# Scan of a gated DeltaNet: QK loaded later and multiplied on GpSimd, KK's beta, the state's decay and the inverse's factor in full width on GpSimd

## The chip, the core and the metric

The kernel runs on one core of a Trainium2 chip. Its engines run side by side, each with its own queue of instructions: TensorE (PE; its weight loads are shown apart as PEld), VectorE (DVE), ScalarE (ACT), GpSimd (POOL), and SyncE (SP), whose queue issues the DMA transfers here. The metric is device time in microseconds (us), the median of several runs. The profile is one further execution, with its own time.

## The reference

One layer of a diffusion backbone, for 128 context tokens and 2048 latent tokens of width 1024. An adaptive RMSNorm feeds one input projection; half of its outputs go through a bidirectional gated DeltaNet with 4 heads of 128, the other half through a gated spatial MLP; an output projection, a residual, a second norm and a squared-ReLU MLP of width 4096 follow. The change lies in the DeltaNet. For each chunk of tokens, direction and head (g is the running sum of the log decays in the chunk, S the state):

```python
decay = where(incl, exp(g[:, None] - g[None, :]), 0)
a_mat = where(strict, (k * beta) @ k.T * decay, 0)
sol   = solve(a_mat + I, concat([v * beta, k * beta * exp(g)]))   # gives u and w
qk    = (q @ k.T) * decay
# one step of the scan:
v_new = u - w @ S
o     = (q * exp(g)) @ S + qk @ v_new
S     = S * exp(g_last) + (k * exp(g_last - g)).T @ v_new
```

## The kernel before, in words

The 2176 tokens are 17 tiles of 128. A first part projects all tiles and writes to DRAM what the scan needs: the keys and queries in both layouts (`kT_d`, `kt_d`, `qT_d`), twice the values (`vt_d`), and the products K K^T (`kk_d`) and K Q^T (`qk_d`) of each tile. Small tables stay in SBUF, a column per tile, direction and head: `beta`, `hbeta` (half of beta), `gcol` (g), `egl` (exp of the last g), `eglg` (exp of the last g less g) and `neg2` (-2 exp g).

The second part is the scan. It has 34 units, 17 tiles forward and then 17 backward, each over one tile of 128 tokens (the kernel takes the tile as the chunk) and all four heads at once, so that a working tile is 128 x 4 x 128, that is 128x512. A unit has two halves.

- The preparation (`prep`, 17 steps) makes the inverse. E is the matrix of decays: ScalarE takes absolute differences of g (L1019) and an exponential (L1020); GpSimd selects the strict triangle Es (L1022) and the inclusive one E (L1024). VectorE multiplies KK by beta and Es, one head at a time (L1032), and GpSimd sets the diagonal to one (L1034). AH and AL are the 16-bit parts of the result. X and Y are the inverse and its transpose, which five levels (block sizes 2 to 32) build up: in each, four small matmuls (L1064), VectorE's masked copy P (L1068), eight small matmuls (L1076, L1078), and ScalarE's two copies to Y and X (L1079, L1080). In the second step of the first level VectorE multiplies QK by E (L1082). A last level and a correction R (L1114) follow, and ScalarE copies the result T from PSUM with the factor half beta, one head at a time (L1123).
- The scan proper (`scan`, 4 steps) is serial from unit to unit through the state S. Step 1: S times kT, which VectorE scales by `neg2` and adds to vt (L1135), and S times qT, which ScalarE scales by `neg2` into o (L1127). Step 2: T times vt; VectorE makes vs with `eglg` (L1148) and ScalarE the copy vn (L1150). Step 3: kt times vs; VectorE makes the new state, S times `egl` plus the product, one head at a time (L1162). Step 4: QK times vn; VectorE joins it with o times -0.5 (L1179, and in the backward pass also with the forward output `of`, L1181).

Between these stand long matmuls that don't depend on the scan, the "fill": in the forward pass the projections of the gated MLP, with GELU and statistics on ScalarE and VectorE; in the backward pass the output projection, its normalisation, and the operands of the later MLP (tiles `opH`, `opL`, L888 and L889). Both need an inverse square root now and then, a power on GpSimd (L183: `rs` in the forward pass, `rr` and `r` in the backward one), with VectorE ahead of it (L182) and behind it.

Each step has a due time in units, a number that `at` and `spread` give it from the list `WINDOWS`; the steps are emitted in the order of these times, and extra edges (`emit`) keep fill matmuls behind those of the chain. The framework then puts each engine's instructions in one order with a planner that has costs of its own. On the chip every engine takes its own in that order, and an instruction that waits holds up those behind it. `prep_loads` (due three units ahead) loads g, KK and QK; `scan_loads` (one unit ahead) loads kt, kT, vt and qT. A tile comes from a ring of buffers with a tag; a load waits until the last reader of its buffer is done. KK, E and Es share one ring of four (`s32`); QK has three of its own; kt, kT, vt, qT and S two each.

The third part is the MLP, some 5,600 long matmuls back to back; the change doesn't touch it.

Of the kernel before, what the change touches and what calls it, by code (L numbers as in the profile page):

```python
# [8 lines left out]
F32 = mybir.dt.float32  # L9
# [3 lines left out]
AF = mybir.ActivationFunctionType  # L13
# [4 lines left out]
P = 128  # L18
# [3 lines left out]
NT = 17  # L22
# [41 lines left out]
def hybrid_step(  # L64
# [53 lines left out]
    make_identity(nc, ident)  # L118
    ident16 = cp.tile([P, P], F16, name="ident16")
    V.tensor_copy(ident16, ident)  # L120
    nhalf = cp.tile([P, 80], F32, name="nhalf")
    V.memset(nhalf, -0.5)
    zcol = cp.tile([P, KT], F32, name="zcol")
    V.memset(zcol, 0.0)
# [31 lines left out]
    neg2 = cp.tile([P, NT, 8], F32, name="neg2")  # L156
    eglg = cp.tile([P, NT, 8], F32, name="eglg")
    egl = cp.tile([P, NT, 8], F32, name="egl")
    vec = cp.tile([P, 73], F32, name="vec")
    a1 = cp.tile([P, 2, KT], F32, name="a1")  # L160
    b1 = cp.tile([P, 2, KT], F32, name="b1")
# [118 lines left out]
    with ExitStack() as ph:  # L280
# [365 lines left out]
        def decay_steps():  # L646
# [46 lines left out]
            def f3():  # L693
                pl = pt()
                T.matmul(pl[:, 0:136], ones, s8(6).rearrange("p t c -> p (t c)"), start=True, stop=True)
                pl3 = pl[:, 0:136].rearrange("p (t c) -> p t c", c=8)
                A.activation(egl, pl3, AF.Exp)
                V.scalar_tensor_tensor(out=eglg, in0=gcol, scalar=-1.0, in1=pl3, op0=ALU.mult, op1=ALU.add)
                A.activation(eglg, eglg, AF.Exp)
                A.activation(neg2, gcol, AF.Exp)  # L700
                V.tensor_scalar_mul(neg2, neg2, -2.0)

            def f4():
                gflat = gcol.rearrange("p t c -> p (t c)")
# [240 lines left out]
    with ExitStack() as ph:  # L945
# [39 lines left out]
        def unit(t, d):  # L985

            u = {}
            sg = 1 if d == 0 else -1

            def col(tab, h):  # L990
                return tab[:, t, d * 4 + h : d * 4 + h + 1]

# [4 lines left out]
            def prep_loads():  # L997
                u["gb"] = load_rows(g_d, t, d)
                u["KK"] = s32("KK")
                load(out=u["KK"], in_=kk_d[t])  # L1000
                u["QK"] = q32("QK", 3)
                load(out=u["QK"], in_=qk_d[t])

            def scan_loads():
                for nm, src in (("kt", kt_d), ("kT", kT_d), ("vt", vt_d), ("qT", qT_d)):
                    u[nm] = q32(nm, 2)
                    if nm in ("kT", "qT"):
                        load(out=u[nm], in_=src[t])
                    else:
                        load(out=u[nm], in_=src[t * P : (t + 1) * P, :].rearrange("p (h d) -> p h d", h=H))  # L1010

            prep = []
            scan = []

            @prep.append
            def _():
                e = s32("E")
                for h in range(H):
                    A.activation(e[:, h, :], u["gb"][:, h, :], AF.Abs, scale=-1.0, bias=col(gcol, h))  # L1019
                A.activation(e, e, AF.Exp, scale=-1.0)  # L1020
                es = s32("Es")
                G.affine_select(out=es, in_=e, pattern=[[0, 4], [-sg, P]], compare_op=ALU.is_gt, fill=0.0,  # L1022
                                base=0, channel_multiplier=sg)
                G.affine_select(out=e, in_=e, pattern=[[0, 4], [sg, P]], compare_op=ALU.is_ge, fill=0.0,  # L1024
                                base=0, channel_multiplier=-sg)
                u["Es"], u["E"] = es, e

            @prep.append
            def _():
                a = u["KK"]  # L1030
                for h in range(H):
                    V.scalar_tensor_tensor(out=a[:, h, :], in0=a[:, h, :], scalar=col(beta, h),  # L1032
                                           in1=u["Es"][:, h, :], op0=ALU.mult, op1=ALU.mult)
                G.affine_select(out=a, in_=a, pattern=[[0, 4], [1, P]], compare_op=ALU.not_equal, fill=1.0,  # L1034
                                base=0, channel_multiplier=-1)
                u["AH"], u["AL"], u["X"] = f16("AH", BA), f16("AL", BA), f16("X", BX)
                A.copy(u["AH"], a)
                V.tensor_tensor(out=u["X"], in0=u["AH"], in1=bc4(bd2), op=ALU.mult)
# [10 lines left out]
            def level(s):  # L1049
# [20 lines left out]
                @prep.append  # L1070
                def _():
                    p = pd()
                    py, px = packed(p, 0), packed(p, 1)
                    y, x, pm = half(u["Y"], yi), half(u["X"], 1 - yi), half(u["P"], yi)
                    for h in range(H):
                        T.matmul(py[:, h], u["X"][:, h, :], pm[:, h], start=True, stop=True)  # L1076
                    for h in range(H):
                        T.matmul(px[:, h], u["P"][:, h, :], x[:, h], start=True, stop=True)  # L1078
                    A.copy(y, py)  # L1079
                    A.copy(x, px)  # L1080
                    if s == 2:
                        V.tensor_tensor(out=u["QK"], in0=u["QK"], in1=u["E"], op=ALU.mult)  # L1082

            for s in (2, 4, 8, 16, 32):
                level(s)
# [31 lines left out]
            @prep.append  # L1117
            def _():
                p = pd()
                quad(p, u["X"], u["R"])  # L1120
                u["T"] = q32("T", BT)
                for h in range(H):
                    A.activation(u["T"][:, h, :], p[:, h, :], AF.Copy, scale=col(hbeta, h))  # L1123

            def scaled(out, p, table):
                for h in range(H):
# [3 lines left out]
            def _():  # L1130
                if u["s"] is not None:
# [5 lines left out]
                    p = pd()  # L1137
                    quad(p, u["qT"], u["s"])
                    u["o"] = q32("o", 2)
                    scaled(u["o"], p, neg2)  # L1140

            @scan.append
            def _():
                p = pd()
                quad(p, u["T"], u["vt"])
                u["vs"] = q32("vs", 1)
                cols = eglg[:, t, d * 4 : d * 4 + 4].unsqueeze(2).to_broadcast([P, 4, P])
                V.tensor_tensor(out=u["vs"], in0=p, in1=cols, op=ALU.mult)  # L1148
                u["vn"] = q32("vn", BT)
                A.copy(u["vn"], p)  # L1150

            @scan.append
            def _():
                s = u["s"]
                p = pd()
                quad(p, u["kt"], u["vs"])
                sn = q32("S", 2)
                if s is None:
                    A.copy(sn, p)
                else:  # L1160
                    for h in range(H):
                        V.scalar_tensor_tensor(out=sn[:, h, :], in0=s[:, h, :], scalar=col(egl, h),  # L1162
                                               in1=p[:, h, :], op0=ALU.mult, op1=ALU.add)
                u["sn"] = sn

            @scan.append
            def _():
# [8 lines left out]
                        V.tensor_tensor(out=o, in0=p, in1=of, op=ALU.add)  # L1176
                else:
                    o = u["o"]
                    V.scalar_tensor_tensor(out=o, in0=o, scalar=-0.5, in1=of if d else p, op0=ALU.mult, op1=ALU.add)  # L1179
                    if d:  # L1180
                        V.tensor_tensor(out=o, in0=o, in1=p, op=ALU.add)  # L1181
                if d == 0:
                    store(out=of_d[t * P : (t + 1) * P, :].rearrange("p (h d) -> p h d", h=H), in_=o)

            u["t"], u["d"] = t, d
            u["prep"], u["scan"] = prep, scan
            u["prep_loads"], u["scan_loads"] = prep_loads, scan_loads
            return u

        units = [unit(t, 0) for t in range(NT)] + [unit(t, 1) for t in [0] + list(range(NT - 1, 0, -1))]  # L1190
# [205 lines left out]
        for i, u in enumerate(units):  # L1396
            w = p2 if i <= NT else p3
            at(i - 3 if i > PL else -10, u["prep_loads"])
            at(i - 1, u["scan_loads"])
            n = len(u["prep"])  # L1400
            for j, st in enumerate(u["prep"]):
                at(i - w[0] + (j + 0.5) * (w[0] - w[1]) / n, st, "prep")
# [556 lines left out]
```

## Time and profile before

| | |
|---|---|
| Median of 3 runs | 2599.12 us (2596.32 to 2601.89) |
| Profiled execution | 2598.87 us, its span 2596.8 us, granted TensorE clock 0.995 |
| First part | 0 to about 440 us |
| Scan, forward pass | about 440 to 880 us |
| Scan, backward pass | about 880 to 1250 us |
| MLP | about 1250 to 2597 us |

A row of a group reads: line, engine, operation, output<-inputs by the program's names, output shape<-input shape, count | busy us, mean ns of one | idle us of the engine just before them, and what ended most of it. A row of waits reads: who waited, for whom, us in total, times, the longest. A row of the timeline reads: start, duration, engine, line, operation, and in brackets the idle time before it and what ended it. Busy matmuls are pipelined, and their ends are modelled. "Busy" of a group merges what overlaps.

### The profile page before, as it was taken

Reading aid. Unit: us, or ns where it says so; the run is one execution under the profiler, and the core shown is the slowest. Engines: PE = TensorE matmul, PEld = TensorE weight load, DVE = VectorE, ACT = ScalarE, POOL = GpSimd, SP = SyncE. Lnnn points to the kernel's source line nnn. Section 1 sums busy time; section 2 is a strip of 40 time slices with the busy share of each in tenths; the row PEclk is TensorE's granted clock in tenths of the full one; section 3 lists DMA queues with packets and bytes.
Section 4 is the critical chain, followed back from the end, with each engine's and each line's share of the span. In section 5 each row is a group of like instructions: output and inputs, shape, how many; then the busy total and the mean of one; then the engine's idle time right before and its main releaser. Section 6 shows DMA issues by size and latency. Waiting matters only on the chain.

```text
span 2596.8 us, 44648 instructions
## 1 busy us (share of the span) xinstructions
PE 2553.3 (98%) x15508; PEld 2156.5 (83%) x15508; DVE 1801.0 (69%) x3733; ACT 1220.9 (47%) x3048; POOL 228.8 (9%) x448
## 2 busy tenths in 40 slices
PE   9999999899999999999999999999999999999998
PEld 5999999688888787778888888888888888888887
DVE  5867756766667878886678876666665557784874
ACT  4755555554555667764355643332342432243441
POOL 3112212111111111210000000000000000000000
PEclk9999999899999999999999999999999999999999
DMA  8977738645445657885768789444479979786773
GB/s 288 304 212 214 209 109 266 201 148 154 154 144 166 208 173 248 275 275 181 279 204 256 224 283 307 114 118 118 123 234 370 334 268 321 270 256 213 236 247 106
DMA packets 494695, 571.88 MB, mean 220 GB/s; under 512 B 35124, under 2 KB 297564, under 8 KB 490886
## 3 DMA queue, kind: packets, MB, share of 16 engines
q1 hardware_dynamic: 494470, 569.04, 68.2%
q8 instruction: 122, 2.00, 0.3%
q14 instruction: 103, 0.84, 0.1%
HBM read 389.23 MB, written 179.67 MB: 219 GB/s over the span
## 4 chain that ended last, share of the span: by engine, by line
PE 87%; DVE 5%; DMA 4%; ACT 1%; issue 1%; POOL 0%; SPq 0%; DVEq 0%; POOLq 0%; ACTq 0%
PE f L226 16%; PE f L228 16%; PE f L227 16%; PE pj L226 7%; PE pj L228 7%; PE pj L227 7%; PE pd L995 5%; PE f L1599 2%; PE pm L226 1%; PE pm L227 1%; PE pm L228 1%; PE pt L610 1%; PE pt L569 1%; DMA QK<-qk_d 1%; PE pd L1076 1%
## 5 line engine op out<-in xcount | busy, mean ns | idle before, releaser
L226 PE MATMUL f<-hop,zH 128*128 128x512 f32 x960 | 373.4, 389 | 1.2 <-ACT zH L1485 1.2
L228 PE MATMUL f<-hop,zL 128*128 128x512 f32 x960 | 373.4, 389 | 0.4 <-DVE zL L1479 0.4
L227 PE MATMUL f<-hop,zH 128*128 128x512 f32 x960 | 373.3, 389 | 0.0
L226 PE MATMUL f<-hop,wH 128*128 128x512 f32 x896 | 355.2, 397 | 0.3 <-DMA hop<-hop_d 0.3
L227 PE MATMUL f<-hop,wH 128*128 128x512 f32 x896 | 349.1, 390 | 0.0
L228 PE MATMUL f<-hop,wL 128*128 128x512 f32 x896 | 347.9, 390 | 0.0
L1485 ACT CAST zH<-zraw 128x512 fp32r<-128x512 f32 x240 | 147.2, 620 | 300.6 <-DMA zraw<-s_d 98.0
L226 PEld LDWEIGHTS f<-hop,zH 128*128 128x128 f32 x960 | 180.2, 188 | 39.2 <-ACT zH L1485 1.6
L228 PEld LDWEIGHTS f<-hop,zL 128*128 128x128 f32 x960 | 180.2, 188 | 38.5 <-DVE zL L1479 1.3
L227 PEld LDWEIGHTS f<-hop,zH 128*128 128x128 f32 x960 | 180.2, 188 | 37.6 <-issue 0.2
L1479 DVE TENSOR_TENSOR zL<-zraw,zH 128x512 fp32r<-128x512 f32 x240 | 162.8, 687 | 65.5 <-ACT zH L1485 51.0
L228 PEld LDWEIGHTS f<-hop,wL 128*128 128x128 f32 x896 | 168.2, 188 | 35.3
L226 PEld LDWEIGHTS f<-hop,wH 128*128 128x128 f32 x896 | 168.5, 188 | 33.0 <-issue 0.7
L227 PEld LDWEIGHTS f<-hop,wH 128*128 128x128 f32 x896 | 168.5, 188 | 32.4
L226 PE MATMUL pj<-kH,wH 128*128 128x386 f32 (+2 forms) x568 | 191.2, 339 | 1.2 <-ACT junk L586 1.1
L228 PE MATMUL pj<-kH,wL 128*128 128x386 f32 (+2 forms) x568 | 190.4, 336 | 0.0
L227 PE MATMUL pj<-kL,wH 128*128 128x386 f32 (+2 forms) x568 | 190.1, 336 | 0.1
L183 POOL TENSOR_TENSOR r<-rsq,nhalf 128x1 f32<-128x1 f32 (+1 forms) x38 | 25.5, 670 | 1428.8 <-DVE rsq L182 1428.8
L556 DVE SCALAR_TENSOR_TENSOR cv<-pj,vec,cv 128x384 f32<-128x384 f32 (+2 forms) x164 | 87.0, 539 | 53.5 <-ACT cv L553 52.2
L226 PEld LDWEIGHTS pj<-kH,wH 128*128 128x128 f32 x568 | 107.6, 190 | 4.3 <-issue 2.3
L227 PEld LDWEIGHTS pj<-kL,wH 128*128 128x128 f32 x568 | 108.0, 190 | 1.1 <-POOL kL L495 0.4
L1485 ACT CAST wH<-s 128x512 fp32r<-128x512 f32 x96 | 59.4, 621 | 104.8 <-DVE s L1479 102.9
(398 smaller groups left out, 5705.5 us busy)
## 6 DMA issues: line engine op xcount, KB each, us to landing
zraw<-z_d SPq DMA_DIRECT2D x212, 256.0 KB
raw<-in_w_ff_dram SPq DMA_DIRECT2D x128, 256.0 KB
hop<-hop_d SPq DMA_DIRECT2D x28, 1024.0 KB
z_d<-c SPq DMA_DIRECT2D x96, 256.0 KB
zraw<-s_d SPq DMA_DIRECT2D x96, 256.0 KB
raw<-in_w_mod_dram SPq DMA_DIRECT2D x80, 256.0 KB
r<-in_w_ff_dram SPq DMA_DIRECT2D x80, 256.0 KB
s_d<-s SPq DMA_DIRECT2D x64, 256.0 KB
```

The source lines that it names most:

```text
L183: G.tensor_tensor(out=out, in0=t[:np_, :n], in1=nhalf[:np_, :n], op=ALU.pow)
L226: T.matmul(ps, lh, rh, start=first and i == 0, stop=False, skip_group_check=more)
L227: T.matmul(ps, lh, rl, start=False, stop=False, skip_group_check=more)
L228: T.matmul(ps, ll, rh, start=False, stop=last and i == n - 1, skip_group_check=more)
L556: V.scalar_tensor_tensor(out=cv[:, o : o + m], in0=ps[:, s + sh : s + sh + m], scalar=convw[:, w, j : j + 1], in1=cv[:, o : o + m], op0=AL ...
L569: T.transpose(pq[:, i * P : (i + 1) * P], u["x2"][:, i * P : (i + 1) * P], ident)
L610: T.matmul(ps[:, i * P : (i + 1) * P], kTt[:, i * P : (i + 1) * P], rhs[:, i * P : (i + 1) * P], start=True, stop=True)
L995: T.matmul(p[:, h, :], lhs[:, h, :], rhs[:, h, :], start=True, stop=True)
L1076: T.matmul(py[:, h], u["X"][:, h, :], pm[:, h], start=True, stop=True)
L1479: V.tensor_tensor(out=out, in0=a, in1=b, op=op)
L1485: A.copy(h, src)
L1599: T.matmul(ps[:, c : c + P], self.raw[m, kh][:, kp, :], x0[kh][:, kp, :], start=first and kp == 0, stop=last and kp == 3)
```

## The change

- QK is loaded in `scan_loads`, one unit ahead and first in that group, instead of three units ahead, with two buffers instead of three.
- A new step `scale_loads`, due 0.6 units ahead, multiplies vt by half beta and QK by E, both on GpSimd. QK's product on VectorE in the first level of the inverse goes.
- KK is multiplied by beta on GpSimd in the first step of the preparation, ahead of Es; VectorE then multiplies it by Es in one instruction of full width instead of four.
- T is copied without a factor, in one ScalarE instruction instead of four; the factor is in vt, and in `neg2`, which becomes -2 exp(g) times half beta. A new table `egc` holds exp(g), with which o is scaled, so that the factor -0.5 in step 4 goes.
- The state's decay is a GpSimd product into the new state's buffer in step 2; step 3 then adds the matmul's result in one VectorE instruction instead of four.
- E has three buffers of its own, and the ring of four holds KK and Es alone.
- The constant `nhalf` is 104 columns wide instead of 80.

```diff
-    nhalf = cp.tile([P, 80], F32, name="nhalf")
+    nhalf = cp.tile([P, 104], F32, name="nhalf")
...
-                A.activation(neg2, gcol, AF.Exp)
-                V.tensor_scalar_mul(neg2, neg2, -2.0)
+                A.activation(egc, gcol, AF.Exp)
+                V.scalar_tensor_tensor(out=neg2, in0=egc, scalar=-2.0, in1=hbeta, op0=ALU.mult, op1=ALU.mult)
...
+            def times(out, src, tab):
+                cols = tab[:, t, d * 4 : d * 4 + 4].unsqueeze(2).to_broadcast([P, 4, P])
+                G.tensor_tensor(out=out, in0=src, in1=cols, op=ALU.mult)
...
                 load(out=u["KK"], in_=kk_d[t])
-                u["QK"] = q32("QK", 3)
+
+            def scan_loads():
+                u["QK"] = q32("QK", 2)
                 load(out=u["QK"], in_=qk_d[t])
-
-            def scan_loads():
...
+            def scale_loads():
+                times(u["vt"], u["vt"], hbeta)
+                G.tensor_tensor(out=u["QK"], in0=u["QK"], in1=u["E"], op=ALU.mult)
...
-                e = s32("E")
+                e = pp.tile([P, 4, P], F32, tag="E", name="E", bufs=3)
...
                 A.activation(e, e, AF.Exp, scale=-1.0)
+                times(u["KK"], u["KK"], beta)
...
-                for h in range(H):
-                    V.scalar_tensor_tensor(out=a[:, h, :], in0=a[:, h, :], scalar=col(beta, h),
-                                           in1=u["Es"][:, h, :], op0=ALU.mult, op1=ALU.mult)
+                V.tensor_tensor(out=a, in0=a, in1=u["Es"], op=ALU.mult)
...
-                    if s == 2:
-                        V.tensor_tensor(out=u["QK"], in0=u["QK"], in1=u["E"], op=ALU.mult)
...
-                for h in range(H):
-                    A.activation(u["T"][:, h, :], p[:, h, :], AF.Copy, scale=col(hbeta, h))
+                A.copy(u["T"], p)
...
-                    scaled(u["o"], p, neg2)
+                    scaled(u["o"], p, egc)
...
+                u["sn"] = q32("S", 2)
+                if u["s"] is not None:
+                    times(u["sn"], u["s"], egl)
...
-                    for h in range(H):
-                        V.scalar_tensor_tensor(out=sn[:, h, :], in0=s[:, h, :], scalar=col(egl, h),
-                                               in1=p[:, h, :], op0=ALU.mult, op1=ALU.add)
-                u["sn"] = sn
+                    V.tensor_tensor(out=sn, in0=sn, in1=p, op=ALU.add)
...
-                    V.scalar_tensor_tensor(out=o, in0=o, scalar=-0.5, in1=of if d else p, op0=ALU.mult, op1=ALU.add)
                     if d:
-                        V.tensor_tensor(out=o, in0=o, in1=p, op=ALU.add)
+                        V.tensor_tensor(out=o, in0=o, in1=of, op=ALU.add)
+                    V.tensor_tensor(out=o, in0=o, in1=p, op=ALU.add)
...
             at(i - 1, u["scan_loads"])
+            at(i - 0.6, u["scale_loads"])
```

More of the change, by code (lines that the diff above doesn't have):

```diff
@@ L158, in hybrid_step @@
     egl = cp.tile([P, NT, 8], F32, name="egl")
+    egc = cp.tile([P, NT, 8], F32, name="egc")
     vec = cp.tile([P, 73], F32, name="vec")
@@ L1156, in _ @@
                 quad(p, u["kt"], u["vs"])
-                sn = q32("S", 2)
+                sn = u["sn"]
                 if s is None:
@@ L1186, in unit @@
             u["prep"], u["scan"] = prep, scan
-            u["prep_loads"], u["scan_loads"] = prep_loads, scan_loads
+            u["prep_loads"], u["scan_loads"], u["scale_loads"] = prep_loads, scan_loads, scale_loads
             return u
```

## The prediction

> **What bounds the kernel now.** I read the page's engine summary first, then the table of stretches, then TensorE's waits inside the scan, and then went upstream from those waits. The first fence is the page, the second the table of stretches (us; busy time of PE, PEld, DVE, ACT, POOL; granted clock; DMA share; GB/s).
>
> ```profile
> span 2596.8 us, 44648 instructions
> PE 2553.3 (98%) x15508; PEld 2156.5 (83%) x15508; DVE 1801.0 (69%) x3733; ACT 1220.9 (47%) x3048; POOL 228.8 (9%) x448
> ```
>
> ```profile
> 480.00:880.00 400.00, 392.83 (x3399) 325.78 (x3398) 280.13 (x786) 214.26 (x583) 50.41 (x69) 1.00 0.52 160
> 880.00:1200.00 320.00, 303.76 (x2717) 251.28 (x2716) 260.11 (x650) 212.70 (x661) 52.70 (x59) 0.99 0.70 230
> 1200.00:1250.00 50.00, 50.00 (x314) 42.29 (x313) 31.51 (x74) 18.26 (x59) 3.45 (x3) 1.00 0.49 170
> 1250.00:2590.00 1340.00, 1336.41 (x6207) 1113.42 (x6205) 906.94 (x1478) 506.43 (x965) 16.06 (x25) 1.00 0.72 235
> ```
>
> TensorE is busy 98% of the span, and the MLP (1250 to 2590) is full. The change touches only the scan, 480 to 1250. There TensorE is idle 7.2 us in the forward pass (400 - 392.83) and 16.2 us in the backward pass (320 - 303.76). VectorE is busy 70% of the first and 81% of the second, ScalarE 54% and 66%, GpSimd 13% and 16%. So the change is worth what it takes from, or adds to, TensorE's waits, and nothing else. They are, from 440 to 1250 (total us, times, longest):
>
> ```profile
> PE pd L1076 <- DVE P L1068: 11.1, 13, 1.6
> PE pd L1064 <- ACT Y L1079: 8.1, 12, 1.5
> PE pd L995 <- issue: 2.4, 1, 2.4
> PE pm L227 <- DVE wL L201: 2.0, 1, 2.0
> PE pd L1076 <- DVE vt L1135: 1.4, 1, 1.4
> ```
>
> The matmuls of the inverse's levels wait 11.1 us for a VectorE product (P) and 8.1 us for a ScalarE copy (Y): 19.2 us in 25 waits, 0.7% of the kernel. That is the stake. Why P and Y are late shows the timeline of a typical stretch of the backward pass (start and duration in us; first VectorE, then ScalarE, then GpSimd and TensorE, whose brackets hold the idle time before):
>
> ```profile
> 1050.89 0.68 DVE L1082 TENSOR_TENSOR QK<-QK,E 128x512 f32<-128x512 f32 x1
> ...
> 1053.04 0.68 DVE L1179 SCALAR_TENSOR_TENSOR o<-o,of 128x512 f32<-128x512 f32 x1
> 1053.64 0.61 DVE L182 TENSOR_SCALAR rsq<-r 128x4 f32<-128x4 f32 x1
> 1054.26 0.81 DVE L1032 SCALAR_TENSOR_TENSOR KK<-KK,beta,Es 128x128 f32<-128x128 f32 x1
> 1054.99 0.68 DVE L889 TENSOR_TENSOR opL<-y,opH 128x512 fp32r<-128x512 f32 x1
> 1055.59 0.87 DVE L1032 SCALAR_TENSOR_TENSOR KK<-KK,beta,Es 128x128 f32<-128x128 f32 x3
> 1056.38 0.74 DVE L1068 TENSOR_TENSOR P<-pd,sm 128x256 f16<-128x256 f32 x2
> ```
>
> ```profile
> 1050.29 1.15 ACT L1123 ACTIVATE T<-pd,hbeta 128x128 f32<-128x128 f32 x4
> 1051.29 0.66 ACT L888 CAST opH<-y 128x512 fp32r<-128x512 f32 x1
> 1051.79 0.42 ACT L1079 CAST Y<-pd 128x256 f16<-128x256 f32 x1
> ```
>
> ```profile
> 1051.71 2.51 POOL L1022 TENSOR_SCALAR_AFFINE_SELECT Es<-E 128x512 f32<-128x512 f32 x1 [9.09 <-DVE QK L1082]
> 1052.27 0.28 PE L1064 MATMUL pd<-Y,AH 128*128 128x64 f16 x4 [0.81 <-ACT Y L1079]
> 1056.85 0.29 PE L1076 MATMUL pd<-P,X 128*128 128x64 f16 x4 [1.39 <-DVE P L1068]
> ```
>
> VectorE works without a gap here, and P stands at the end of the queue, behind two things that the change takes or shortens (QK at 1050.89, KK at 1054.26 and 1055.59). Y stands two places behind T on ScalarE.
>
> **The change, part by part.** The prices are these groups (mean ns of one behind the busy us):
>
> ```profile
> L1032 DVE SCALAR_TENSOR_TENSOR KK<-KK,beta,Es 128x128 f32<-128x128 f32 x136 | 45.8, 390 | 9.0 <-POOL Es L1022 7.2 <-DMA KK<-kk_d 1.7
> L1162 DVE SCALAR_TENSOR_TENSOR S<-S,egl,pd 128x128 f32<-128x128 f32 x128 | 35.8, 340 | 9.6 <-PE pd L995 9.5
> L1082 DVE TENSOR_TENSOR QK<-QK,E 128x512 f32<-128x512 f32 x34 | 23.5, 690 | 31.9 <-DMA QK<-qk_d 29.0 <-POOL E L1024 2.7
> L1148 DVE TENSOR_TENSOR vs<-pd,eglg 128x512 f32<-128x512 f32 x34 | 23.1, 679 | 5.5 <-PE pd L995 5.5
> L1179 DVE SCALAR_TENSOR_TENSOR o<-o,of 128x512 f32<-128x512 f32 x16 | 11.8, 739 | 1.0 <-ACT o L1127 1.0
> L1123 ACT ACTIVATE T<-pd,hbeta 128x128 f32<-128x128 f32 x136 | 38.8, 376 | 0.5 <-PE pd L995 0.5
> L1150 ACT COPY vn<-pd 128x512 f32<-128x512 f32 x34 | 20.2, 593 | 40.4 <-DVE vs L1148 40.3
> L1022 POOL TENSOR_SCALAR_AFFINE_SELECT Es<-E 128x512 f32<-128x512 f32 x34 | 26.2, 772 | 310.1 <-DVE QK L1082 181.5 <-ACT E L1020 68.9 <-DVE mv L1245 20.9
> L1024 POOL TENSOR_SCALAR_AFFINE_SELECT E<-E 128x512 f32<-128x512 f32 x34 | 23.5, 690 | 2.2
> L183 POOL TENSOR_TENSOR rr<-rsq,nhalf 128x4 f32<-128x4 f32 x17 | 18.4, 1080 | 140.5 <-DVE rsq L182 140.5
> L183 POOL TENSOR_TENSOR rq<-rsq,nhalf 128x68 f32<-128x68 f32 x1 | 11.2, 11246 | 16.2 <-DVE rsq L182 16.2
> ```
>
> VectorE, per unit. KK: four instructions, 45.8/34 = 1.35 us, become one full-width product like QK's, 0.69: saves 0.66. QK's product leaves: saves 0.69. The state: 35.8/32 = 1.12 us becomes one addition from PSUM like vs, 0.68: saves 0.44. The output keeps its instructions; the backward one falls from 739 to about 690 ns, 0.05 in half of the units. Sum 1.8 us per unit, 61 us in 34. VectorE also stops waiting for QK's transfer, 29.0/34 = 0.85 us per unit. What is late next there is P's own matmul, not another transfer.
>
> ScalarE, per unit: T falls from 38.8/34 = 1.14 us to one copy from PSUM like vn, 0.59: saves 0.55.
>
> GpSimd, per unit, gains four products 128x512: KK by beta, vt by half beta, QK by E, the state by its decay (the last not in the first unit of a pass). No row has one. From below it can't be cheaper than a one-input pass over the same shape, 0.69 us (L1024). From above stands only the power at 128x68, 11.2 us, 165 ns a column or 84 us for 512: I leave that end out, because it is another operation, and L1024 streams 512 columns in 0.69. The nearest is L1024 with a second operand to stream, 2 x 0.69 = 1.38 us (an estimate), and I take it; four make 5.5 us. GpSimd's busy time goes from (50.41 + 52.70 + 3.45)/34 = 3.1 us per unit to 8.6, in a period of about 22 us. It doesn't become the bound. The Trainium skill, GPSIMD Engine Reference, section "Performance versus the Vector engine", has 4497 ns for a two-input product of 2048 columns: that would be 1.12 us for one and 4.5 us for four, which no run here shows and which leaves the time as it is.
>
> The order on GpSimd. Each product stands in a queue with Es, E, KK and the powers (rr, rs). KK's product comes ahead of Es, while ScalarE makes E, so it is covered; that cover ends only if kk_d is late. Behind vt's and QK's products wait later powers: a power meets a new product 5.5/22 = 25% of the time, for half of 1.38 us, 0.17 us each. For 17 rr and 17 rs that is 6 us of delay to VectorE, of which I charge a quarter to TensorE, 1.5 us. The state's product needs only the state of the unit before, most of a period ahead of its addition.
>
> The transfers. QK has two buffers instead of three and is loaded two units later. A load goes out when a matmul has freed its buffer, as these issues show:
>
> ```profile
> 705.87 0.38 SPq L1010 DMA_DIRECT2D kt<-kt_d  x1
> ...
> 709.73 0.32 SPq L1008 DMA_DIRECT2D kT<-kT_d  x1
> ...
> 710.83 0.38 SPq L1008 DMA_DIRECT2D qT<-qT_d  x1
> 715.03 0.32 SPq L1002 DMA_DIRECT2D QK<-qk_d  x1
> ```
>
> So QK's load should still go out near 715, for the next unit instead of the one after it, and is used most of a period later: no cost. If SP took it ahead of kt, kT and qT, it would hold them back up to 715.03 - 705.87 = 9.2 us of their period of 22; between 0 and that I take 0, since each is issued as its own buffer comes free. E gets three buffers of its own, so Es no longer waits for QK's product to free a slot (181.5 us of GpSimd's idle time); what it waits for next is E itself (68.9). That lets KK start sooner, but it is GpSimd's idle time and I count nothing. The two setup instructions run once.
>
> The shared interface. In the stretch above Es takes 2.51 us where L1024 has 0.69: it began while VectorE ran instructions with two SBUF operands back to back, and ended with them. Then rsq, four columns, took 0.61 us, and one KK 0.81 instead of the 0.34 that its shape takes in L1162: 0.47 us of waiting for a GpSimd pass of 0.69. So a pass twice as long stalls VectorE 0.9 us when it collides. In the backward pass I let one in two collide (0.45 us per product), in the forward pass, where VectorE is idle twice as often, one in four. The Trainium skill states a rule for it (SBUF — State Buffer, section "Who interferes with whom"): a VectorE instruction with two SBUF inputs and a GpSimd instruction that reads SBUF exclude each other for the whole instruction. By that rule, with which these rows agree, part of the relief is lost again; by a plain sum of busy times the gain would be 13 us.
>
> The sum. In the stretch P's queue loses QK (0.61 start to start) and about 0.64 of KK, 1.25 us. It gets back 8.4 us of queue / 22 x 4 products x 0.45 = 0.7. So 0.55 of the 1.39 us goes, 40%; of 11.1 us, 4.4. Y's waits average 8.1/12 = 0.68 us, T ends 0.55 sooner, but other casts lie between: 60% of 8.1, 4.9. Less 1.5 for the powers: **7.8, so 8 us less**. Against the profiled execution's 2598.87 us (its span is 2596.8) that is 2591; the median of the three runs, 2599.12, lies 0.25 us away. From no change I could tell 0.2%, 5 us.
>
> **Rivals.** First, *the lock decides, slower*. If every product in the backward pass collides and holds VectorE for its whole 1.38 us, 14 units x (4 x 1.38 - 1.8 - 0.85) = 40 us are added to the 260.11 of 320: VectorE is at 94%, and P's and vt's waits double, 12.5 us more: 2611. It decides from 0.66 us of stall per product on, where the stalls eat the relief, (1.8 + 0.85)/4. For it: DVE is 81% busy there and the stalls stand in the rows. Against: a GpSimd pass more often waits for VectorE than the reverse (2.51 against 0.46).
>
> Second, *the powers queue*: products that wait for vt's or QK's transfer, or for VectorE, hold rr and rs back by a whole product, 34 x 1.38 = 47 us; a quarter reaches TensorE, 12, against 4.4 + 4.9 saved: 2602, and with a wait per product like Es's 2.51, 2606. For it: the 0.85 us that QK now waits moves to GpSimd. Against: GpSimd has 60% left.
>
> Third, *no change*: TensorE's waits are where the written order puts a consumer just behind its producer; with shorter producers the order closes up again and the same 25 waits of 0.77 us return elsewhere: 2599. For it: 11.1 us over 13 different places. Against: the work leaves the very queues that end last.
>
> **How the numbers follow.** Forecast 0.52, lock 0.18, powers 0.12, no change 0.18. Faster 0.52, slower 0.30, same 0.18. The forecast's own range is 2580 (all 19.2 us gone) to 2594. The whole range takes in the lock's 2611 and a little below the floor: 2577 to 2612.
>
> **What would show it.** Right: T about 0.59 and KK's product about 0.69 per unit, S's addition 0.68; no DVE wait for QK's transfer; VectorE's busy time from 480 to 1250 lower by 40 to 60 us; L1064's and L1076's waits down to about 10 us; GpSimd's products near 1.38 us. Wrong: products far above 1.4 us, DVE's two-operand instructions longer, DVE waiting for rr or rs, TensorE waiting for vt, S or QK where it waited for none, or the time coming from the MLP, which nothing here touches.

## The result, and the profile after

The change makes the kernel slower: 2611.41 us (2608.37 to 2614.39) against 2597.92 us for the kernel before on the same chip, a ratio of 1.0054 [1.0041, 1.0067], about 14 us. The forecast was 2591. The page of the changed kernel begins:

```profile
span 2609.6 us, 44479 instructions
PE 2563.5 (98%) x15508; PEld 2155.3 (83%) x15508; DVE 1774.6 (68%) x3501; ACT 1204.7 (46%) x2946; POOL 390.6 (15%) x582
```

VectorE and ScalarE are less busy, by 26 and 16 us, GpSimd more busy by 162, and the span is 12.8 us longer. The same number of matmuls keeps TensorE busy 10.2 us longer (2563.5 against 2553.3). The table of stretches, with the same columns and stretches as before, says where:

```profile
480.00:880.00 400.00, 393.91 (x3415) 325.16 (x3414) 261.34 (x668) 205.28 (x531) 129.90 (x134) 1.00 0.50 159
880.00:1200.00 320.00, 301.11 (x2695) 250.73 (x2694) 248.55 (x553) 207.51 (x615) 118.56 (x115) 0.98 0.69 228
1200.00:1250.00 50.00, 50.00 (x318) 42.48 (x317) 30.90 (x67) 16.51 (x53) 5.73 (x5) 1.00 0.50 174
1250.00:2590.00 1340.00, 1338.80 (x6164) 1106.08 (x6163) 901.91 (x1468) 504.94 (x964) 16.02 (x24) 1.00 0.71 234
```

The last row holds the surprise. TensorE is full in the MLP before and after, at the same granted clock of 1.00, yet in the same 1340 us it starts 6164 matmuls instead of 6207. The forecast had the MLP as untouched. The MLP's first long matmul starts 1.1 us later than before (at 1255.91 against 1254.85), and from there to the start of its last one the MLP takes 1344.9 us instead of 1333.1. So 11.8 of the 12.8 us arise in the MLP, and one in all that comes ahead of it.

The scan gained nothing either. TensorE's waits from 440 to 1250 us after the change:

```profile
PE pd L1072 <- ACT Y L1087: 13.1, 14, 2.1
PE pd L1084 <- DVE P L1076: 6.5, 4, 3.6
PE pd L1000 <- DVE R L1120: 3.8, 4, 1.6
PE pm L228 <- DVE wL L202: 3.5, 2, 2.8
PE pd L1000 <- DMA S<-in_state_delta_dram: 1.9, 1, 1.9
```

The wait for P fell from 11.1 to 6.5 us. The one for Y rose from 8.1 to 13.1, and R, which took 0.3 us before, now takes 3.8. The groups that the change touched (line, engine, operation, output<-inputs, shapes, count | busy us, mean ns | idle before it and its releasers):

```profile
L1128 ACT COPY T<-pd 128x512 f32<-128x512 f32 x34 | 20.2, 593 | 4.6 <-PE pd L1000 4.6
L1041 DVE TENSOR_TENSOR KK<-KK,Es 128x512 f32<-128x512 f32 x34 | 27.0, 795 | 20.9 <-POOL Es L1032 13.6 <-POOL KK L993 7.2
L1169 DVE TENSOR_TENSOR S<-S,pd 128x512 f32<-128x512 f32 x32 | 21.8, 680 | 9.5 <-PE pd L1000 9.5
L993 POOL TENSOR_TENSOR KK<-KK,beta 128x512 f32<-128x512 f32 x34 | 36.6, 1077 | 24.9 <-DMA KK<-kk_d 24.9
L993 POOL TENSOR_TENSOR vt<-vt,hbeta 128x512 f32<-128x512 f32 x34 | 38.0, 1118 | 49.7 <-DMA vt<-vt_d 30.6 <-DVE oL L1341 7.2 <-PE pd L1100 3.7
L993 POOL TENSOR_TENSOR S<-S,egl 128x512 f32<-128x512 f32 x32 | 34.4, 1076 | 61.8 <-DVE S L1169 56.6 <-DMA out_dram<-S 5.2
L1019 POOL TENSOR_TENSOR QK<-QK,E 128x512 f32<-128x512 f32 x34 | 46.1, 1356 | 217.9 <-DMA QK<-qk_d 196.4 <-PE pd L1086 19.4 <-PE pd L1000 2.1
L1034 POOL TENSOR_SCALAR_AFFINE_SELECT E<-E 128x512 f32<-128x512 f32 x34 | 32.8, 966 | 1.8
L1028 ACT ACTIVATE E<-gb,gcol 128x128 f32<-128x128 f32 x136 | 44.2, 392 | 40.2 <-POOL QK L1019 35.4 <-DMA gb<-g_d 4.8
```

Each instruction costs nearly what the forecast said. New are two things in the last columns: the wait for QK's transfer (29.0 us on VectorE before) is now 196.4 us of GpSimd's time, and ScalarE waits 35.4 us for QK's product before it may begin E (28 times). A stretch of the backward pass shows how that wait can reach TensorE (start and duration in us; GpSimd, ScalarE, ScalarE, TensorE):

```profile
1048.92 1.30 POOL L1019 TENSOR_TENSOR QK<-QK,E 128x512 f32<-128x512 f32 x1 [8.13 <-PE pd L1086]
...
1050.25 0.99 ACT L1028 ACTIVATE E<-gb,gcol 128x128 f32<-128x128 f32 x3 [0.82 <-POOL QK L1019]
...
1051.96 0.35 ACT L1087 CAST Y<-pd 128x256 f16<-128x256 f32 x1
...
1052.36 0.28 PE L1072 MATMUL pd<-Y,AH 128*128 128x64 f16 x4 [2.08 <-ACT Y L1087]
```

E's buffer comes free only when the QK product of an earlier unit ends (in the compiled program, that of three units before). ScalarE stands 0.82 us for it, Y is in the queue behind E, and TensorE waits 2.08 us for Y. That stretch suggested a cause for the rise at Y, and the experiments below test whether it is the price.

### The profile page after: what moved, and what is told of

Its sections match the earlier page's. It is cut to its first block, busy times and chain, and to the rows that moved or that the text cites. A ratio compares the mean times of both kernels' runs of the same rounds, so it can differ in the third digit from the quotient of the medians.

```text
span 2609.6 us, 44479 instructions
## 1 busy us (share of the span) xinstructions
PE 2563.5 (98%) x15508; PEld 2155.3 (83%) x15508; DVE 1774.6 (68%) x3501; ACT 1204.7 (46%) x2946; POOL 390.6 (15%) x582
## 4 chain that ended last, share of the span: by engine, by line
PE 90%; DMA 4%; DVE 2%; ACT 2%; issue 1%; POOL 1%; SPq 0%; DVEq 0%; POOLq 0%; ACTq 0%
PE f L227 16%; PE f L229 16%; PE f L228 16%; PE pj L227 7%; PE pj L229 7%; PE pj L228 7%; PE pd L1000 5%; PE f L1605 2%; PE pm L227 2%; PE pm L228 2%; PE pm L229 2%; DMA QK<-qk_d 1%; PE pt L611 1%; PE pt L570 1%; PE pd L1072 1%
```

## The experiments

Each ratio is to the kernel before on the same chip, with its 95% interval.

**1. Is the MLP's loss a matter of where things lie?** The change makes `nhalf` 24 columns wider (96 bytes per partition) and adds `egc` (17 x 8 values, 544 bytes). By the addresses in the compiled program, all tiles that are laid out from the left edge of SBUF lie 640 bytes further right, the MLP's weight tiles (pool `wp`) among them. The pool `hopA`, two of the seven tiles that feed the MLP's moving operand, lies at the right edge and stays. Modulo 512 bytes, the weights and `hopA` both lie at 384 before; after the change the weights lie at 0 and `hopA` at 384. The kernel before with nothing but a wider constant:

```diff
-    nhalf = cp.tile([P, 80], F32, name="nhalf")
+    nhalf = cp.tile([P, 240], F32, name="nhalf")
```

> The kernel before, with the constant nhalf 240 columns wide instead of 80 and nothing else: every buffer allocated after it from the left moves by 640 bytes, as in the changed kernel; the two hop tiles at the right end of SBUF stay. Theory L (layout): in the changed kernel the MLP's long matmuls are slower (1340 us become about 1352) because weights and moving operand now stand otherwise to each other, so this kernel shows 2598 + 11.7 = about 2610 us, its matmuls with a moving operand in the right-hand hop tiles start every 233 ns instead of 227, and its scan is as before. Rival W (the scan's work reaches into the MLP, by the order of transfers or the clock): about 2598 us and 227 ns.

Measured: 2608.88 us, 1.0058 [1.0046, 1.0071]. Its last stretch has the row of the changed kernel, though not an instruction of the change is in it:

```profile
1250.00:2590.00 1340.00, 1338.81 (x6164) 1106.09 (x6163) 900.67 (x1469) 504.34 (x964) 15.91 (x24) 1.00 0.70 234
```

So the shift alone costs about what the whole change costs. The opposite test, the change with the shift made a multiple of 512 bytes (640 + 384 = 1024), and the change with the left side as it is and the right edge moved by 384 bytes instead:

```diff
-    nhalf = cp.tile([P, 104], F32, name="nhalf")
+    nhalf = cp.tile([P, 200], F32, name="nhalf")
```

> The changed kernel with nhalf 200 columns wide instead of 104: the shift against the kernel before is 1024 bytes instead of 640, so weights and moving operands stand to each other as before modulo 512. Theory L: the MLP is back at its length, 2611.4 - 11.7 = about 2600 us, and what is left against before, some 1 to 4 us, is the scan's own account. Rival W: about 2611 us.

```diff
-    pick = edge.tile([P, 12, 2], F32, name="pick")[:, 0:2, :]
+    pick = edge.tile([P, 60, 2], F32, name="pick")[:, 0:2, :]
```

> The changed kernel with the small tile at the right end 480 bytes instead of 96, so the right-hand hop tiles move down by 384 bytes; nothing on the left moves. Theory L, if the distance between the two operands modulo 512 is what counts: about 2600 us, as with the shift by 1024. If the weights' own address counts: about 2611 us. Rival W: about 2611 us.

Measured: 1.0012 [1.0003, 1.0021] and 0.9999 [0.9991, 1.0008]. Both give the MLP back; the last stretch, in the kernel with the moved right edge:

```profile
1250.00:2590.00 1340.00, 1335.01 (x6202) 1112.84 (x6201) 907.02 (x1477) 506.50 (x967) 16.38 (x26) 1.00 0.70 235
```

Since a left shift of 1024 and a right-edge shift of 384 both mend it, neither the address of the weights nor that of the moving operand is at fault, but the distance between them (both cures bring the two 1024 bytes nearer than before). All left-hand tiles move together; that the partner is the weights is inferred, since they are what TensorE reads beside the moving operand.

The two mended kernels hold the same instructions, and only their places and the planner's order of some of them differ; yet their ratios lie 0.13% apart. A difference of that size between two of the kernels below can't be put down to an edit.

Another distance, with a left shift of 544 bytes (distance 32):

```diff
-    nhalf = cp.tile([P, 104], F32, name="nhalf")
+    nhalf = cp.tile([P, 80], F32, name="nhalf")
```

> The changed kernel with nhalf at its old 80 columns: shift 544 bytes, that is 32 modulo 512 instead of 128. Theory L, if any other distance is as bad: about 2611 us; if only whole steps of 128 collide: about 2600 us, or something between. Rival W: about 2611 us.

Measured: 1.0039 [1.0024, 1.0055], with 6158 matmuls in the last stretch. A distance of 32 is as bad as 128. What happens is seen matmul by matmul. In the changed kernel, at the point where the moving operand changes from a left-hand tile to one of `hopA` (start and duration in us):

```profile
1979.94 0.39 PE L227 MATMUL f<-hop,zH 128*128 128x512 f32 x1
1980.17 0.39 PE L228 MATMUL f<-hop,zH 128*128 128x512 f32 x1
1980.40 0.39 PE L229 MATMUL f<-hop,zL 128*128 128x512 f32 x1
...
1981.32 0.39 PE L227 MATMUL f<-hop,zH 128*128 128x512 f32 x1
1981.55 0.40 PE L228 MATMUL f<-hop,zH 128*128 128x512 f32 x1
1981.79 0.39 PE L229 MATMUL f<-hop,zL 128*128 128x512 f32 x1
1982.01 0.40 PE L227 MATMUL f<-hop,zH 128*128 128x512 f32 x1
1982.25 0.39 PE L228 MATMUL f<-hop,zH 128*128 128x512 f32 x1
```

From start to start it is 0.23 us in the first three (226 or 227 ns in the unrounded times), and in the last five it is 229 and 238 ns by turns (to one ns). Over the whole MLP the mean from start to start, in stretches without a gap, with the moving operand in one of the two `hopA` tiles:

| kernel | distance of weights and `hopA`, mod 512 | `hopA` tiles, ns | left-hand tiles, ns |
|---|---|---|---|
| before | 0 | 227.1, 226.8 | 226.8 to 227.0 |
| changed | 128 | 232.6, 232.9 | 226.8 to 227.9 |
| before, shifted by 640 | 128 | 232.6, 232.9 | 226.8 to 227.9 |
| changed, shift 544 | 32 | 233.4, 233.4 | 226.8 to 228.2 |
| changed, shift 1024 | 0 | 227.1, 226.8 | 226.8 to 227.0 |
| changed, right edge moved | 0 | 227.0, 226.8 | 226.8 to 227.1 |

Some 1950 such intervals (967 + 987) times 5.8 ns are 11.3 us, nearly all of the MLP's loss of 11.8; the left-hand tiles rise by up to 1 ns as well, which stays unexplained. The left-hand tiles always move with the weights, so their distance stays 0 modulo 512 in all six.

**2. What part of the change undoes the gain in the scan?** From here on the changed kernel has its right edge moved as above, so that the MLP has its old length; its ratio of 0.9999 (1.0012 with the other cure) is the scan's own account: nothing gained, where 8 us were forecast. First, all of the change but QK's part (QK loaded three units ahead with three buffers, multiplied on VectorE in the first level, E back in the shared ring):

```diff
             def prep_loads():
...
+                u["QK"] = q32("QK", 3)
+                load(out=u["QK"], in_=qk_d[t])
...
-                u["QK"] = q32("QK", 2)
-                load(out=u["QK"], in_=qk_d[t])
...
-                G.tensor_tensor(out=u["QK"], in0=u["QK"], in1=u["E"], op=ALU.mult)
...
-                e = pp.tile([P, 4, P], F32, tag="E", name="E", bufs=3)
+                e = s32("E")
...
+                    if s == 2:
+                        V.tensor_tensor(out=u["QK"], in0=u["QK"], in1=u["E"], op=ALU.mult)
```

> The whole QK part undone: loaded three units ahead with three buffers, multiplied by E on VectorE in the first level, E in the ring with KK and Es; the other parts (KK's beta, vt's half beta, the state's decay on GpSimd, full width) stay. Theory R: the other parts keep their gain, 2598 - 5 on the scale of the first forecast, here about 2591 us. Rival G: three products are left of four, and the time is 2596 us or more. Should the QK part be the one with the gain (VectorE's waits for its transfer), it is above 2596.

And the reverse, the kernel before with QK's part alone (these lines the other way round, and the step `scale_loads` with QK's product only):

> The kernel before with the QK part alone: loaded one unit ahead with two buffers, its product on GpSimd 0.6 units ahead, E in three buffers of its own. Theory R: ScalarE's E waits for the product as in the changed kernel and TensorE for Y; VectorE is relieved of 0.69 us and of its wait for the transfer, 1.5 us a unit; the two about cancel or it is slower, 2596 to 2601 us. Rival G: one product of four, 2594 us.

Measured: without QK's part 2591.61 us, **0.9983 [0.9974, 0.9992]**, faster than both kernels; QK's part alone 1.0005 [0.9994, 1.0015]. TensorE's two first waits, without QK's part, and then with QK's part alone (with ScalarE's new wait):

```profile
PE pd L1083 <- DVE P L1075: 11.2, 16, 1.8
PE pd L1071 <- ACT Y L1086: 4.7, 8, 1.7
```

```profile
PE pd L1067 <- ACT Y L1082: 17.1, 18, 3.3
PE pd L1079 <- DVE P L1071: 6.2, 7, 1.9
...
ACT E L1022 <- POOL QK L1013: 34.2, 25, 3.5
```

So the parts can be told apart. KK, T, vt and the state's decay bring Y's wait from 8.1 to 4.7 and leave P's where it was (11.2); QK's part takes 5 us from P and adds 9 to Y. Together with QK's part nothing is left of 4.1 us. Each wait comes from one execution: in the kernel before with the wider constant, whose scan has the same instructions, P takes 13.8 and Y 7.0 us, so 2 or 3 us of a wait say little.

The waits aren't the only channel. The mean granted clock over the runs on one chip is 0.9966 in the kernel before, 0.9961 without QK's part and 0.9944 with QK's part alone; on another it is 0.9965 before and 0.9956 in the changed kernel with its right edge moved. Had TensorE been busy whenever its clock was below one, 0.0022 would be 5.7 us and 0.0009 2.3 us (estimates, from these shares of 2596 us). No run holds the clock fixed, so how much of QK's price goes this way stays open.

**3. Does ScalarE's wait for QK's product make Y late?** If so, a kernel without that wait should have the gain of both. Four kernels tried to remove it by buffers or time. A fourth buffer for E (`gb` gives one up for it):

```diff
-            gb = q32("gb", 2)
+            gb = q32("gb", 1)
...
-                e = pp.tile([P, 4, P], F32, tag="E", name="E", bufs=3)
+                e = pp.tile([P, 4, P], F32, tag="E", name="E", bufs=4)
```

> All from here on with the right-hand tiles moved as in a_edge, so the MLP has its old length and the time is the scan's own account; a_edge took 2595.8 us, the kernel before 2595.7. This one gives E four buffers instead of three, and gb one instead of two to make room. Theory R (ring): ScalarE's E waits 35 us, 27 times, for GpSimd's QK product to free E's buffer, and the copies Y queue behind it; with a fourth buffer that wait goes, TensorE's wait for Y falls from 11.9 us to about 6, and the time to about 2590 us. Rival G (GpSimd's products hold VectorE at the shared interface, and that eats the gain): ScalarE's wait goes, but the time stays at 2596 us. Rival B: gb with one buffer makes E wait for its load instead, 2596 us or more, which the waits would show.

Measured: 1.0009 [0.9999, 1.0020]. The wait stays, although in the compiled program E now waits for the product of four units before instead of three:

```profile
ACT E L1028 <- POOL QK L1019: 38.3, 27, 3.8
```

ScalarE's own E in a tile that only the two selects read, with the inclusive select going into a ring of three, in the changed kernel and in the kernel with QK's part alone:

```diff
-            gb = q32("gb", 2)
+            gb = q32("gb", 1)
...
-                e = pp.tile([P, 4, P], F32, tag="E", name="E", bufs=3)
+                e = pp.tile([P, 4, P], F32, tag="E0", name="E0", bufs=1)
+                ei = pp.tile([P, 4, P], F32, tag="E", name="E", bufs=3)
...
-                G.affine_select(out=e, in_=e, pattern=[[0, 4], [sg, P]], compare_op=ALU.is_ge, fill=0.0,
+                G.affine_select(out=ei, in_=e, pattern=[[0, 4], [sg, P]], compare_op=ALU.is_ge, fill=0.0,
...
-                u["Es"], u["E"] = es, e
+                u["Es"], u["E"] = es, ei
```

> As a_edge, but ScalarE writes E into a tile of its own (one buffer), from which GpSimd selects both triangles, the inclusive one into the ring of three that the QK product frees; gb has one buffer to make room. So ScalarE needs nothing that the QK product frees; what waits for that product is GpSimd's own next select, which stands behind it in any case. The fourth buffer didn't help because the planner then made E earlier by as much (ScalarE still waited 38 us, 27 times). Theory R, in its new form (ScalarE's queue, with the copies Y in it, waits for GpSimd's QK product because E's buffer hangs on it): ScalarE's wait for QK's product is gone, TensorE's wait for Y falls from 11.9 us to about 5, as in a_noqk (4.7), its wait for P stays at about 6, and the time is 2588 to 2591 us. Rival G (the products' stalls at the shared interface eat the gain): 2596 us. Rival T (TensorE waits for something else of the QK part, R or S): in between, with those waits in the list.

> As b_qkonly, with E split in the same way. b_qkonly took 2596.1 us with 17.1 us of waiting for Y and 6.2 for P. Theory R: the wait for Y falls to about 8 as in the kernel before, P stays near 6, and the time is 2588 to 2592 us. Rival G: 2595 us or more.

Measured: 1.0012 [1.0003, 1.0021] and 0.9994 [0.9985, 1.0003]. ScalarE now waits for the select instead, 34.0 and 38.1 us, and Y takes 12.1 and 14.2 us: little changed but the name of the releaser. And QK loaded three units ahead again (three buffers, `gb` one), with the product still on GpSimd:

> QK is loaded three units ahead into three buffers again, as in the kernel before, but its product stays on GpSimd; gb has one buffer to make room. Theory R: the product no longer waits for a load that only just got its buffer (182 us of GpSimd's idle time), so E's buffer is freed in time: ScalarE's wait below 10 us, about 2590 us. Rival G: 2596 us.

Measured: 1.0017 [1.0005, 1.0030]; ScalarE waits 36.2 us for the product, Y takes 8.3, P 8.5 and R 4.2 us. None of these four removes the wait, so they leave the question open. That the planner moves E forward as far as its buffer lets it would explain why; it was not tested. With one buffer for `gb`, ScalarE also waits for g (from 440 to 1250 us, 9.8 us in the last of them and 2.0 in the changed kernel), which none of these runs separates.

**4. The engine, or the late load?** The changed kernel with QK's product on VectorE, and all else of the change kept:

```diff
-                G.tensor_tensor(out=u["QK"], in0=u["QK"], in1=u["E"], op=ALU.mult)
+                V.tensor_tensor(out=u["QK"], in0=u["QK"], in1=u["E"], op=ALU.mult)
```

> As a_edge, but the QK product, still 0.6 units ahead with the late load, on VectorE instead of GpSimd. Theory R: E's buffer now hangs on a VectorE product of 0.69 us that waits for QK's transfer; ScalarE still waits for it, less per time than the 1.3 us now, so Y's waits are between 5 and 12 us, and P's are back near 11, because VectorE has the product and the wait for the transfer again: 2593 to 2598 us. If the place on GpSimd is the whole fault and the late load none: as a_noqk, 2591.6.

Measured: 0.9996 [0.9987, 1.0005]. ScalarE waits for that product too, Y takes 9.3 and P 13.0 us:

```profile
ACT E L1028 <- DVE QK L1019: 32.6, 22, 4.3
```

Then the kernel without QK's part, with its one product moved from VectorE to GpSimd at its old place, and the kernel with the early load and that old place, but with E's own ring and one buffer for `gb`:

```diff
                     if s == 2:
-                        V.tensor_tensor(out=u["QK"], in0=u["QK"], in1=u["E"], op=ALU.mult)
+                        G.tensor_tensor(out=u["QK"], in0=u["QK"], in1=u["E"], op=ALU.mult)
```

> As a_noqk (2591.61 us: QK's load, buffers and place as before the change, all else as in the change), with the one product moved from VectorE to GpSimd at its place. Theory W: no wait of ScalarE for QK's product, so Y stays at 4 to 6 us, P falls from 11.2 towards 7 since VectorE's queue is 0.69 us shorter per unit, and the time is 2586 to 2592. Theory L: the lock and GpSimd's queue make it slower than a_noqk, 2595 to 2600, with Y above 8.

> QK is loaded three units ahead again and its product stays on GpSimd, but stands where VectorE's stood before the change (in the level s = 2 of the unit's own preparation), so it ends more than a unit before the product in the change does; E keeps its own ring of three, gb has one buffer, the layout is that of a_edge. Only the place of the product differs from a_qkearly (2600.25 us; ScalarE waits 36.2 us for QK's product, TensorE 8.3 for Y, 8.5 for P, 4.2 for R). Theory W (the late product holds E's buffer, ScalarE stands in front of Y and R for it): ScalarE's wait for the product falls below 10 us, Y falls to 4 to 6, R to 1, and the time to 2588 to 2593. Theory L (a product of 1.3 us on GpSimd costs what it costs by the lock and the queue, wherever it stands): Y and P together stay above 15, the time at 2596 to 2601, even where ScalarE's wait is gone.

Measured: 1.0026 [1.0015, 1.0036] and 1.0024 [1.0012, 1.0037]. In the second ScalarE's wait is still there (35.5 us), so it says nothing on that. The first tells more. ScalarE doesn't wait for the product at all in it, and yet the move of this one product costs 0.43%, some 11 us, against 0.9983. Its waits: TensorE's two first, and VectorE's for GpSimd (the last row is GpSimd's own):

```profile
PE pd L1083 <- DVE P L1075: 16.8, 14, 3.1
PE pd L1071 <- ACT Y L1086: 5.9, 12, 1.7
...
DVE KK L1040 <- POOL Es L1031: 20.9, 16, 2.8
...
DVE vg L1258 <- POOL rs L184: 11.1, 10, 2.3
...
POOL QK L1089 <- DMA QK<-qk_d: 148.6, 19, 12.5
```

With the product on VectorE the third and the fourth row read 7.8 and 6.6 us:

```profile
DVE KK L1040 <- POOL Es L1031: 7.8, 8, 3.2
DVE vg L1258 <- POOL rs L184: 6.6, 7, 1.1
```

GpSimd stands up to 12.5 us for QK's transfer, with Es next behind it in its queue:

```profile
1004.67 1.29 POOL L1089 TENSOR_TENSOR QK<-QK,E 128x512 f32<-128x512 f32 x1 [6.92 <-DMA QK<-qk_d]
1006.03 1.15 POOL L1031 TENSOR_SCALAR_AFFINE_SELECT Es<-E 128x512 f32<-128x512 f32 x1
```

So VectorE, rid of a product of 0.73 us per unit, waits 13.1 us more for Es and 4.5 more for rs, and P becomes later, not earlier (16.8 against 11.2). Put side by side, by the engine of the product and the load:

| | product on VectorE | product on GpSimd |
|---|---|---|
| QK loaded three units ahead | 0.9983 | 1.0026, 1.0024, 1.0017 |
| QK loaded one unit ahead | 0.9996 | 0.9999 |

(Above right: at the old place, there with E's own ring, and at the change's place; the last two also have one buffer for `gb`. The two others in the lower row have the change's place and ring.)

That ScalarE's wait is the whole price has fallen: without it, the move of the product still costs 11 us. That it is no part of the price isn't shown. With it and with VectorE's product the kernel stands at 0.9996, 0.13% above 0.9983, which is no more than the two mended kernels lie apart. In the change, with its late load, the product costs about the same on both engines (0.9996 and 0.9999), so what takes the gain there, GpSimd's queue or the late load with E's own ring, stays open.

Where the 11 us arise is seen in part. From 440 to 1250 us TensorE is idle for 32.4 us instead of 25.6 (810 less its busy time of 777.60 and 784.40), which is 6.8 of the 10.4 us between these two profiled executions; P has 5.6 of it. The rest isn't explained, and the planner's order differs in each of these kernels.

The best kernel of the study is the change without QK's part and with the right edge moved: 0.17% faster than before, where the change as it stands costs 0.54%.

## Why the prediction was wrong

- **"the time coming from the MLP, which nothing here touches"** is the step that failed, and it decides the sign. The instructions of the MLP are the same; their addresses aren't. "The two setup instructions run once" priced the new tables by their instructions alone, and the wider constant was priced at nothing. The missing term is 640 bytes of layout, +11.8 us, shown by the shift alone (1.0058) and its two cures (0.9999 and 1.0012). The forecast named the MLP as a place that would refute it, but gave no rival for it.
- **The scan, "8 us less"**: measured 0.9999 and 1.0012 with the layout mended, at best 2.3 us less. The parts other than QK's give 4.1 us, about half of the forecast and little more than the 0.13% by which the two mended kernels differ.
- **T and Y's 4.9**: right in mechanism and near in size where QK's part is absent. T took 0.593 us against 0.59, and Y's wait fell by 3.4, as far as one execution tells. In the change itself it rose by 5.0, because of QK's part.
- **P's 4.4**: the wait fell by 4.6, but not for the reason given. KK's shorter product is in the kernel without QK's part, and there P waits 11.2 us, as before. P fell in the kernels that have QK's product on GpSimd and E in a ring of its own (5.7 to 8.5 us), and there Y, and with the other parts R as well, took its time. That is the third rival's mechanism ("the same 25 waits return elsewhere"), to which the forecast gave 0.18.
- **"E gets three buffers ... I count nothing"**: a wait of 35.4 us on ScalarE was the result. It is real, and in the stretch shown it delays TensorE. It isn't needed for QK's product to cost time, since the move costs 11 us without it; whether it is part of the price in the change stays open.
- **"no cost" for QK's load; VectorE "stops waiting for QK's transfer"**: it did, but GpSimd waits in its place (196.4 us), and there the select Es and the powers stand behind it: VectorE's wait for Es goes from 7.2 to 13.6 us, for rs from 4.8 to 10.6. The second rival had this mechanism for the powers and forgot Es. It was priced at 11 to 15 us above the forecast (2602 to 2606), with a chance of 0.12; by its own figures the upper end is 2611 (a quarter of 34 x 2.51 is 21 us, less the 9.3 saved). The product's move alone under the early load cost 11.
- **The lock**: the work removed from VectorE is 61 us by the measured durations (34 x 1.35 + 32 x 0.44 + 16 x 0.05), its busy time from 480 to 1250 fell from 571.75 to 540.79, 31 us, so 30 us came back over 134 products: 0.22 us each, half of the 0.45 that the sum took for the backward pass, and far from the 0.66 at which the first rival decides. That this rival's 2611 us is the measured time is luck: its 12.5 us were to come from P's and vt's waits, and the 11.8 came from the MLP. GpSimd paid as well: the select E takes 966 ns instead of 690. That two operands from SBUF on VectorE and a reading GpSimd instruction hold each other up agrees with the Trainium skill, SBUF — State Buffer, section "Who interferes with whom"; here each side pays a part, on average.
- **GpSimd's 1.38 us**: three products took 1.08 to 1.12, QK's 1.36. The estimate from the select, 1.38, fits QK's, the one with two full operands; the three have a broadcast column as their second. The Trainium skill's figure (GPSIMD Engine Reference, section "Performance versus the Vector engine") is for an addition of two tensors, and the 1.12 us worked out from it is an estimate: the three come near it, and QK's product took more.

## What to carry to other kernels

A change that adds a constant or widens a tile moves everything allocated after it: look at the long matmuls outside the change first, at their count in an equal stretch, and test the shift alone before explaining anything by the instructions. Work taken from a busy engine is worth only what stands behind it on that engine; put on an in-order queue that waits for transfers, a product holds up what the first engine needs next. And when a wait disappears, add up all waits of the bounding engine: here P's 4.6 us came back as Y and R.

## What the runs showed of the hardware

The pace of back-to-back 128x512 matmuls depended on how the weights and the moving operand lie to each other in SBUF: 227 ns from start to start where their addresses agreed modulo 512 bytes, 233 ns on average where they differed by 32 or 128 (229 and 238 by turns at 128), at a granted clock of 1.00 in both. Only these distances were tried, so a smaller step than 512, such as 256, may do as well; and the weights moved with all other left-hand tiles. The Trainium skill, TensorE: Matmul & The Clock Gate, section "Step-by-step: what each phase is for", has it that loading the next weights takes no SBUF read bandwidth from the running matmul; these runs show a loss of 2.6% that goes with the relative address, and don't show its mechanism.
